# Both products of a decoder's MLP by Strassen's seven block products, with the activations between them kept in DRAM

## The chip, the cores and the metric

The kernel runs on one core of a Trainium2 chip. The metric is the device time of one execution in microseconds (us), the median of three runs; less is better.

## The reference

One layer of a decoder: model width 1024, 1024 tokens, hidden width 4096, all float32. The mixers at its front are the same before and after, and only what follows them matters here:

```
x = x + mix @ w_out                       # (1024,1024) @ (1024,1024)
h2 = rms_norm(x, norm2_g)
x = x + square(relu(h2 @ w_ff1)) @ w_ff2  # 1024x1024 @ 1024x4096, then 1024x4096 @ 4096x1024
```

## The kernel before

**Precision.** TensorE multiplies a reduced format, so each float32 operand is split in two: a "hi" part, a cast that ScalarE (ACT) does, and a "lo" part, the operand minus hi, a subtraction that VectorE (DVE) or GpSimd (POOL) does. Each product is three matmuls, hi by hi, lo by hi and hi by lo (`mm3`, L160 to L162). A matmul has a 128x128 stationary operand and a 128x512 moving one, and its result goes to a PSUM bank of 128x512.

**Output projection and second norm.** `wo_tile` makes a 128-token, 512-column tile of the projection in PSUM (`po`) and adds x. The first column half is done in two parts: seven of eight row blocks early, under the last attention unit, and the eighth at the end, added to what lies in SBUF. Then `norm_to_T` normalises the tile (a short chain of small operations), scales it (`n2sq`, L150), transposes it on TensorE (`n2tp`, L153) and splits it (ACT L156, DVE L157) into `h2Th`, `h2Tl`. Tokens come in eight tiles t; "half 0" is t of 0 to 3, "half 1" the rest. x1, the residual, stays in 16 SBUF tiles.

**MLP.** `ff1(fi, half)` makes one block of 128 hidden columns for 512 tokens: 8 by 3 matmuls into `pf`, relu and square on ACT (L947, L948), r times r and the lo part on DVE (L949, L950). `ff2(c)` takes two such blocks and makes 16 output tiles `py`, 6 matmuls each, that DVE adds into x1 (L963). First and second product alternate, chunk by chunk, 16 chunks in all; the first four blocks of half 0 (`EARLY`) have no use for half 1, and a scheduler that orders the program puts their matmuls between the last steps of the second norm. Weights come in 256 KB pieces on SP's queue (`w1raw`, `w2raw`); ACT makes hi (L119) and POOL lo (L122). The two products have 1536 matmuls each.

## Time and profile before

| | |
|---|---|
| median of 3 runs | 1412.03 us (1410.52 to 1413.05) |
| profiled execution, span | 1414.0 us |
| busy: TensorE (PE), DVE, ACT, POOL | 96%, 58%, 41%, 31% |
| last `po` matmul starts | 711.24 us |
| last `n2tp` transposes start | 723.70 us |

The span is that of one profiled execution, from its first instruction to its last, and is 2.0 us above the median of the timed runs. In rows of the profile a `start us, us, engine line op out<-in` gives start and duration; out and in are tiles by the program's names; brackets give how long the engine sat idle before it and what ended that. "PEclk" is the TensorE clock that was granted, 1.00 being full.

### The profile page before, as it was taken

To read this page: it belongs to the slowest core of one execution; us is meant where nothing else is said; L and a number is where in the kernel's file an instruction comes from. 1 tells how busy PE (TensorE), PEld (TensorE's weight loads), DVE (VectorE), ACT (ScalarE), POOL (GpSimd) and SP (SyncE) were. 2 spreads that over 40 slices of the span, in tenths; PEclk is the share of its full clock that TensorE was granted. 3 is DMA by queue.
4 is the path that set the end of the run, shared out by engine and by line. 5 is a ranking of instruction groups with operands and counts; after the bars stand their busy time and mean duration, and the time that the engine had idled before them with its cause. 6 is when DMAs were issued, how large, how long until landed. Compare 5 with 4: busy or idle time off the path is not lost.

```text
span 1414.0 us, 20140 instructions
## 1 busy us (share of the span) xinstructions
PE 1356.7 (96%) x7584; PEld 1133.8 (80%) x7584; DVE 816.6 (58%) x1623; ACT 578.1 (41%) x1401; POOL 442.0 (31%) x470
## 2 busy tenths in 40 slices
PE   4999989999999898899999999999999999999998
PEld 4978879878698795577888888888888888888887
DVE  6768657868676788968554434334343334334344
ACT  5566436867694457746442112221122211122111
POOL 6213684504126836211032222221122211222210
PEclk9999989999999998999999999999999999999999
DMA  8101220202002112313022112210122111122103
GB/s 222 41 17 28 48 47 16 60 23 60 23 9 68 29 41 77 118 52 98 31 75 60 35 55 60 60 46 30 45 60 60 51 32 43 54 60 60 40 21 119
DMA packets 107305, 76.89 MB, mean 54 GB/s; under 512 B 44220, under 2 KB 85180, under 8 KB 107208
## 3 DMA queue, kind: packets, MB, share of 16 engines
...
## 4 chain that ended last, share of the span: by engine, by line
PE 84%; DVE 8%; DMA 2%; ACT 2%; issue 2%; POOL 1%; SPq 0%; POOLq 0%; DVEq 0%; ACTq 0%
PE pf L162 8%; PE pf L161 8%; PE py L160 8%; PE py L161 8%; PE pf L160 8%; PE py L162 8%; PE pj L160 6%; PE pj L162 6%; PE pj L161 6%; PE av L459 3%; PE atp L440 2%; DVE sbr L398 2%; PE po L160 2%; PE po L161 2%; PE po L162 2%
## 5 line engine op out<-in xcount | busy, mean ns | idle before, releaser
L963 DVE TENSOR_TENSOR x<-py,x 128x512 f32<-128x512 f32 x256 | 176.1, 688 | 304.6 <-PE py L162 304.6
L122 POOL TENSOR_TENSOR w2lo<-w2raw,w2hi 128x512 fp32r<-128x512 f32 x64 | 81.9, 1303 | 440.9 <-ACT w2hi L119 440.9
L162 PE MATMUL pf<-h2Th,w1lo 128*128 128x512 f32 x512 | 199.3, 389 | 0.0
L160 PE MATMUL pf<-h2Th,w1hi 128*128 128x512 f32 x512 | 199.3, 389 | 0.0
L161 PE MATMUL pf<-h2Tl,w1hi 128*128 128x512 f32 x512 | 199.2, 389 | 0.0
L160 PE MATMUL pj<-whi,hTh 128*128 128x384 f32 (+2 forms) x512 | 172.5, 339 | 2.2 <-ACT vg L606 1.2
L161 PE MATMUL pj<-wlo,hTh 128*128 128x384 f32 (+2 forms) x512 | 171.7, 337 | 0.0
L162 PE MATMUL pj<-whi,hTl 128*128 128x384 f32 (+2 forms) x512 | 171.5, 336 | 0.0
L119 ACT CAST w2hi<-w2raw 128x512 fp32r<-128x512 f32 x64 | 36.5, 619 | 251.6 <-PE pf L161 171.9
L949 DVE TENSOR_TENSOR fr<-fr 128x512 f32<-128x512 f32 x64 | 65.8, 1028 | 106.1 <-ACT ah L948 89.8
L947 ACT ACTIVATE fr<-pf 128x512 f32<-128x512 f32 x64 | 38.0, 594 | 200.7 <-PE pf L162 200.7
L122 POOL TENSOR_TENSOR w1lo<-w1raw,w1hi 128x512 fp32r<-128x512 f32 x64 | 81.6, 1301 | 119.8 <-ACT w1hi L119 119.7
L160 PEld LDWEIGHTS pf<-h2Th,w1hi 128*128 128x128 f32 x512 | 96.2, 188 | 19.9
L162 PEld LDWEIGHTS pf<-h2Th,w1lo 128*128 128x128 f32 x512 | 96.1, 188 | 19.9
L161 PEld LDWEIGHTS pf<-h2Tl,w1hi 128*128 128x128 f32 x512 | 96.1, 188 | 19.9
L160 PEld LDWEIGHTS pj<-whi,hTh 128*128 128x128 f32 x512 | 99.2, 194 | 5.7 <-issue 1.7
L161 PEld LDWEIGHTS pj<-wlo,hTh 128*128 128x128 f32 x512 | 99.1, 194 | 2.5 <-issue 1.9
L352 POOL TENSOR_TENSOR qd<-qraw,qnr 128x128 f32<-128x128 f32 x96 | 47.7, 518 | 169.4 <-PE qtp L356 160.1
L162 PEld LDWEIGHTS pj<-whi,hTl 128*128 128x128 f32 x512 | 98.7, 193 | 2.3 <-issue 1.3
L161 PE MATMUL py<-w2lo,ah 128*128 128x512 f32 x256 | 99.6, 389 | 0.0
L162 PE MATMUL py<-w2hi,al 128*128 128x512 f32 x256 | 99.6, 389 | 0.0
L160 PE MATMUL py<-w2hi,a 128*128 128x512 f32 x256 | 99.6, 389 | 0.0
...
## 6 DMA issues: line engine op xcount, KB each, us to landing
w1raw<-in_w_ff_dram SPq DMA_DIRECT2D x64, 256.0 KB, 2.9
w2raw<-in_w_ff_dram SPq DMA_DIRECT2D x64, 256.0 KB, 3.0
...
wraw<-in_w_in_dram SPq DMA_DIRECT2D x16, 256.0 KB, 3.9
xraw<-in_x_dram SPq DMA_DIRECT2D x16, 256.0 KB, 2.8
cb<-c_dram SPq DMA_DIRECT2D x12, 256.0 KB, 3.3
...
mix_m<-ot ACTq DMA_DIRECT2D x10, 256.0 KB, 2.0
```

The costliest lines, as they stand in the source:

```text
L119: S.copy(hi, raw)
L122: lo_eng.tensor_tensor(out=lo, in0=raw, in1=hi, op=ALU.subtract)
L160: PE.matmul(o, lhsT=lh, rhs=rh, start=start, stop=False)
L161: PE.matmul(o, lhsT=lh, rhs=rl, start=False, stop=False)
L162: PE.matmul(o, lhsT=ll, rhs=rh, start=False, stop=stop)
L352: G.tensor_tensor(out=qd[:, :, e, :], in0=st["q"][half][:, ts, h, :], in1=st["r"][half][:, ts, h:h + 1].broadcast_to([P, 2, HD]), op=ALU.mult)
L398: V.tensor_tensor_scan(out=rv, data0=rv, data1=e[:, ::-1], initial=0.0 if prev is None else prev, op0=ALU.add, op1=ALU.add)
L440: PE.transpose(out=tp[:, j * P:(j + 1) * P], in_=a_of[c][:, j * P:(j + 1) * P], identity=ident)
L459: PE.matmul(o[h * HD:(h + 1) * HD, c0:], lhsT=st["v"][j // 4][:, j % 4, h, :], rhs=at[h][j // 4][:, j % 4, c0:], start=(j == 0), stop=(j = ...
L947: S.activation(r, p, AF.Relu)
L949: V.tensor_tensor(out=r, in0=r, in1=r, op=ALU.mult)
L963: V.tensor_tensor(out=x1[(t, ch)], in0=p, in1=x1[(t, ch)], op=ALU.add)
```

## The change

Each of the two MLP products is a 2x2 block product. Strassen's form with 15 sums needs seven block products instead of eight, and sums of blocks before and after them. Tile names change accordingly.

- **Count.** First product: 16 pairs q of hidden blocks, 7 products of 12 matmuls each. Second: 16 pairs q in groups of 1, 3, 4, 4 and 4; a group does its seven products one after the other (order 1, 6, 2, 7, 5, 4, 3), 4 token tiles by n pairs by 3 matmuls each. That is 1344 matmuls for each, 2688 in place of 3072.
- **x1** no longer stays in SBUF. The early part goes to DRAM (`x1p`) and comes back; the finished tiles go to `x1d` (writes on ACT's queue) and come back as 16 tiles `xo` at the start of the second product.
- **Second norm.** `to_ops` writes blocks b11, b21 for half 0 and forms differences with half 1 (four DVE operations for each tile, L978, L968, L971, L969). After the last tile, t1, t4 and b22 are split: 12 ACT casts and 12 DVE subtractions (L999, L1000).
- **First product** (`ff1`). For each q POOL does 4 sums of weight blocks (L1026) and 3 lo's, DVE 4 lo's and 5 additions from PSUM, ACT 7 casts, a copy, 4 relus, 4 squares. Two products, w11 by b11 and w12 by b21, run two pairs ahead. The result goes to DRAM (`yd`, 64 writes of 256 KB on SP's queue, L1040). The second product starts when the first is done.
- **Second product.** The activations (`yraw`) and weights (`w2raw`) come in 512 KB tiles on SP's queue (L1112), 8 buffers each, 4 KB a partition. Both operands of each product are split (`cut`): 2 ACT casts and 2 lo's for each q. In all POOL has 172 operations here (48 lo's L133, 60 additions of `u` into `xo` L1142, 64 sums L1160, L1163, L1165, L1185). DVE has 360: 176 lo's (L133) and 64 sums (L1162, L1164, L1166, L1186), which read two SBUF tiles, and 120 additions that read PSUM. ACT has 244. Split operands have 32 buffers, two products of a group of four.

PE at the end of the second norm. Before, around the transposes of the last two tiles (`pf` is the first MLP product):

```order
L162 MATMUL pf<-h2Th,w1lo 128x512
L160 MATMUL pf<-h2Th,w1hi 128x512
L161 MATMUL pf<-h2Tl,w1hi 128x512
L153 MATMUL n2tp<-ident,n2sq 128x128 x12
L162 MATMUL pf<-h2Th,w1lo 128x512
```

And now, the same place (`pa` is the first MLP product):

```order
L162 MATMUL n2tp<-ident,n2sq 128x128 x8
L173 MATMUL po<-woh,mTh 128x512
L174 MATMUL po<-wol,mTh 128x512
L175 MATMUL po<-woh,mTl 128x512
L162 MATMUL n2tp<-ident,n2sq 128x128 x16
L1033 MATMUL pa<-b11h,w11h 128x512
```

The first MLP product's matmuls stood ahead of the last transposes; now they stand behind them, and nothing is between the last `po` and those transposes.

ACT behind the same place. Now (L977, L964 and L973 belong to `to_ops`; `t_8748`, `t_8757` and `b_8766` are the hi parts of t1, t4 and b22; `w12h` is the second operand that PE needs):

```order
L977 COPY b_8721<-n2tp 128x512
L964 COPY hraw<-n2tp 128x4x128
L999 CAST t_8748<-hraw 128x512 x4
L973 CAST t_8482<-t2f 128x4x128
L973 CAST t_8483<-t3f 128x4x128
L999 CAST t_8757<-hraw 128x512 x4
L999 CAST b_8766<-hraw 128x512 x4
L130 CAST w12h<-w1raw 128x512
```

The casts of the last blocks stand ahead of `w12h`.

POOL at the start of the second product, now (`u` is a block product on its way to the output, `xo` the residual):

```order
L1160 TENSOR_TENSOR s_11222<-yraw 128x512
L1163 TENSOR_TENSOR yraw<-yraw 128x512
L1165 TENSOR_TENSOR yraw<-s_11222,yraw 128x512
L133 TENSOR_TENSOR fbl<-w2raw,fbh 128x512
L1185 TENSOR_TENSOR yraw<-yraw 128x512
L1142 TENSOR_TENSOR xo<-u,xo 128x512 x5
```

The additions into `xo` come early in POOL's order and need the residual back from DRAM. On SP's queue its 16 loads stand behind the last six writes of `yd` and the first four 512 KB loads, and the first addition takes the 13th of them. Of the next group's 16 loads those of `A[q, 1]` and `B[q, 1]` take buffers that this group's last two products still read.

The diff, its core; the MLP section before (`load_ff1` to the end) is removed whole:

```diff
-    sb = ctx.enter_context(tc.tile_pool(name="sb", bufs=1))
...
+    def pool(name, side=None, space=None):
+        kw = dict(space=space) if space else dict(side=side)
+        held[name] = ExitStack()
+        return held[name].enter_context(tc.tile_pool(name=name, bufs=1, reuse_waits="tile", **kw))
+    sb_w = pool("sb_w", "left")
+    sb_a = pool("sb_a", "right")
+    sb_t = pool("sb_t", "right")
+    ps = pool("ps", space=PSUM)
...
-            S.copy(hi[:, ks, sl], pv)
-            V.tensor_tensor(out=lo[:, ks, sl], in0=pv, in1=hi[:, ks, sl], op=ALU.subtract)
+            tT(t, c, p.rearrange("p (k t) -> p k t", t=P))
...
+    x1p = dr.tile([T, 512], F32, name="x1p")
+    x1d = dr.tile([T, D], F32, name="x1d")
     def wo_tile(ch, t, k0, k1):
...
+        ts, cs = slice(t * P, (t + 1) * P), slice(ch * 512, (ch + 1) * 512)
+        xr = big("raw", "xraw")
+        nc.sync.dma_start(out=xr, in_=xf[ts, cs] if k0 == 0 else x1p[ts])
+        if k1 < NK:
+            part = big("xt", "xpart")
+            V.tensor_tensor(out=part, in0=p, in1=xr, op=ALU.add)
+            nc.scalar.dma_start(out=x1p[ts], in_=part)
+        else:
+            x1[(t, ch)] = sb_h.tile([P, 512], F32, name="x1", tag="x1", bufs=4)
+            V.tensor_tensor(out=x1[(t, ch)], in0=p, in1=xr, op=ALU.add)
+            nc.scalar.dma_start(out=x1d[ts, cs], in_=x1[(t, ch)])
...
-        norm_to_T([x1[(t, 0)], x1[(t, 1)]], g2b, h2T, t, "n2")
...
+    held["sb_t"].close()
+    sb_h = pool("sb_h", "right")
...
+    def to_ops(t, c, pv):
+        sl = slice((t % 4) * P, (t % 4 + 1) * P)
+        raw = hraw[c][:, :, sl]
+        if t < 4:
+            hi, lo = (a[:, :, sl] for a in HB[("b11", "b21")[c]])
+            S.copy(hi, pv)
+            V.tensor_copy(raw, pv)
+            G.tensor_tensor(out=lo, in0=raw, in1=hi, op=ALU.subtract)
+            return
+        b22 = hraw[2][:, :, sl]
+        if c == 1:
+            if "t2" not in HB:
+                hop("t2", "a")
+                hop("t3", "a")
+            S.copy(b22, pv)
+            for name in ("t2", "t3"):
+                x = big("zs", name + "f", [P, 4, P])
+                if name == "t2":
+                    V.tensor_tensor(out=x, in0=b22, in1=hraw[0][:, :, sl], op=ALU.subtract)
+                    V.tensor_tensor(out=raw, in0=raw, in1=x, op=ALU.subtract)
+                else:
+                    V.tensor_tensor(out=x, in0=b22, in1=b12[0], op=ALU.subtract)
+                hi, lo = (a[:, :, sl] for a in HB[name])
+                S.copy(hi, x)
+                G.tensor_tensor(out=lo, in0=x, in1=hi, op=ALU.subtract)
+        else:
+            b12[0] = big("zs", "b12", [P, 4, P])
+            S.copy(b12[0], pv)
+            V.tensor_tensor(out=raw, in0=b12[0], in1=raw, op=ALU.subtract)
+    b12 = [None]
+    for t in TORD:
+        wo_tile(0, t, LAST, NK)
+        wo_tile(1, t, 0, NK)
+        norm_to_T([x1.pop((t, 0)), x1.pop((t, 1))], g2b, to_ops, t, "n2")
+    held["sb_w"].close()
+    sb_m = pool("sb_m", "left")
+    held["ps"].close()
+    pb = pool("pb", space=PSUM)
+    def bank(name):
+        return pb.tile([P, 512], F32, name=name, tag="b", bufs=8)
+    for name, raw, side in (("t1", hraw[0], "a"), ("t4", hraw[1], "a"), ("b22", hraw[2], "m")):
+        hop(name, side)
+        hi, lo = HB[name]
+        for k in range(4):
+            S.copy(hi[:, k], raw[:, k])
+            V.tensor_tensor(out=lo[:, k], in0=raw[:, k], in1=hi[:, k], op=ALU.subtract)
+    NPAIR = DFF // P // 2
+    yd = dr.tile([DFF, T], F32, name="yd")
+    AHEAD = 2
...
+    def ff1(q):
+        st = {}
+        def load():
+            home, n = (sb_h, 2) if q % 3 == 0 else (sb_m, 4)
+            st["w"] = [home.tile([P, 4, 2 * P], F32, name="w1raw", tag="wr", bufs=n) for _ in range(2)]
+            for c in range(2):
+                nc.sync.dma_start(out=st["w"][c], in_=w_ff1[c * 512:(c + 1) * 512, q * 2 * P:(q + 1) * 2 * P].rearrange("(k p) c -> p k c", p=P))
+        def blk(i, k):
+            return st["w"][k][:, :, i * P:(i + 1) * P]
+        def comb(name, a, b, op):
+            x = sb_m.tile([P, 4, P], F32, name=name, tag="s", bufs=4)
+            G.tensor_tensor(out=x, in0=a, in1=b, op=op)
+            return x
+        def prod(name, raw, b, eng, o, start=True, first=False):
+            wh, wl = pieces(raw, name, eng, sb_h if first else sb_m, 2 if first else 9)
+            bh, bl = HB[b]
+            for k in range(4):
+                PE.matmul(o, lhsT=wh[:, k], rhs=bh[:, k], start=start and k == 0, stop=False, skip_group_check=not start)
+                PE.matmul(o, lhsT=wh[:, k], rhs=bl[:, k], start=False, stop=False, skip_group_check=not start)
+                PE.matmul(o, lhsT=wl[:, k], rhs=bh[:, k], start=False, stop=k == 3, skip_group_check=not start)
+        def out(i, j, y):
+            f0 = (2 * q + i) * P
+            S.activation(y, y, AF.Square)
+            nc.sync.dma_start(out=yd[f0:f0 + P, j * 512:(j + 1) * 512], in_=y)
+        def one():
+            st["a"] = bank("pa")
+            prod("w11", blk(0, 0), "b11", V, st["a"], first=True)
+            st["c"] = sb_h.tile(BLK, F32, name="cc", tag="hraw", bufs=3)
+            S.copy(st["c"][:, 0], st["a"])
+            prod("w12", blk(0, 1), "b21", V, st["a"], start=False)
+            r = sb_m.tile([P, 512], F32, name="r", tag="r", bufs=1)
+            S.activation(r, st["a"], AF.Relu)
+            out(0, 0, r)
+        def two():
+            c = st["c"]
+            s1 = comb("s1", blk(1, 0), blk(1, 1), ALU.add)
+            s2 = comb("s2", s1, blk(0, 0), ALU.subtract)
+            b_ = bank("pb")
+            prod("s2", s2, "t2", G, b_)
+            V.tensor_tensor(out=c[:, 0], in0=b_, in1=c[:, 0], op=ALU.add)
+            s3 = comb("s3", blk(0, 0), blk(1, 0), ALU.subtract)
+            c_ = bank("pc")
+            prod("s3", s3, "t3", G, c_)
+            V.tensor_tensor(out=c[:, 1], in0=c_, in1=c[:, 0], op=ALU.add)
+            d_ = bank("pd")
+            prod("s1", s1, "t1", V, d_)
+            V.tensor_tensor(out=c[:, 1], in0=d_, in1=c[:, 1], op=ALU.add)
+            s4 = comb("s4", blk(0, 1), s2, ALU.subtract)
+            prod("w22", blk(1, 1), "t4", G, c_, start=False)
+            V.tensor_tensor(out=c[:, 2], in0=c_, in1=c[:, 0], op=ALU.add)
+            prod("s4", s4, "b22", V, d_, start=False)
+            V.tensor_tensor(out=c[:, 3], in0=d_, in1=c[:, 0], op=ALU.add)
+            for n, (i, j) in ((1, (1, 1)), (2, (1, 0)), (3, (0, 1))):
+                S.activation(c[:, n], c[:, n], AF.Relu)
+                out(i, j, c[:, n])
+        return load, one, two
+    steps = [ff1(q) for q in range(NPAIR)]
+    for q in range(AHEAD):
+        steps[q][0]()
+        steps[q][1]()
+    for q in range(NPAIR):
+        if q + AHEAD < NPAIR:
+            steps[q + AHEAD][0]()
+        steps[q][2]()
+        if q + AHEAD < NPAIR:
+            steps[q + AHEAD][1]()
+    held["sb_h"].close()
+    held["sb_a"].close()
+    held["sb_m"].close()
+    sb_f = pool("sb_f", "left")
+    GROUPS = (1, 3, 4, 4, 4)
+    GM = max(GROUPS)
+    X = {}
+    def ft(shape, name, tag, bufs, dt=F32):
+        return sb_f.tile(shape, dt, name=name, tag=tag, bufs=bufs)
+    q0 = 0
+    for gi, n in enumerate(GROUPS):
+        qs = range(q0, q0 + n)
+        q0 += n
+        last = gi == len(GROUPS) - 1
+        A, B = {}, {}
+        for q in qs:
+            for k in range(2):
+                for M, src, nm in ((A, yd, "yraw"), (B, w_ff2, "w2raw")):
+                    M[q, k] = ft([P, 2, 512], nm, nm, 2 * GM)
+                    f0 = (2 * q + k) * P
+                    nc.sync.dma_start(out=M[q, k].rearrange("p a b -> p (a b)"), in_=src[f0:f0 + P, :])
+        if gi == 0:
+            for j in range(2):
+                for i in range(2):
+                    for ti in range(4):
+                        X[ti, i, j] = ft([P, 512], "xo", "xo", 16)
+                        t = i * 4 + ti
+                        nc.sync.dma_start(out=X[ti, i, j], in_=x1d[t * P:(t + 1) * P, j * 512:(j + 1) * 512])
+        ops = {}
+        def cut(m, a, b):
+            for q in qs:
+                l, r = [], []
+                for to, x, nm, eng in ((l, a(q), "fa", V), (r, b(q), "fb", V if m in (1, 2, 5, 7) else G)):
+                    hi, lo = (ft([P, 512], nm + c, "fop", 8 * GM, F32R) for c in "hl")
+                    split(x, hi, lo, eng)
+                    to += [hi, lo]
+                ops[m, q] = l + r
+        def run(m, ti, o, start=True):
+            ts = slice(ti * P, (ti + 1) * P)
+            for q in qs:
+                lh, ll, rh, rl = ops[m, q]
+                kw = dict(skip_group_check=not start)
+                PE.matmul(o, lhsT=lh[:, ts], rhs=rh, start=start and q == qs[0], stop=False, **kw)
+                PE.matmul(o, lhsT=lh[:, ts], rhs=rl, start=False, stop=False, **kw)
+                PE.matmul(o, lhsT=ll[:, ts], rhs=rh, start=False, stop=q == qs[-1], **kw)
+        def add(ti, i, j, y, eng=V):
+            eng.tensor_tensor(out=X[ti, i, j], in0=y, in1=X[ti, i, j], op=ALU.add)
+        def done(ti, i, j):
+            if last:
+                t = i * 4 + ti
+                nc.sync.dma_start(out=outf[t * P:(t + 1) * P, j * 512:(j + 1) * 512], in_=X[ti, i, j])
+        s1, t1, pa, pc, pd, u = {}, {}, {}, {}, {}, {}
+        cut(1, lambda q: A[q, 0][:, 0], lambda q: B[q, 0][:, 0])
+        for ti in range(4):
+            pa[ti] = bank("pa")
+            run(1, ti, pa[ti])
+            u[ti] = ft([P, 512], "u", "u", 4)
+            S.copy(u[ti], pa[ti])
+        for q in qs:
+            s1[q] = ft([P, 512], "s1", "s1", GM)
+            G.tensor_tensor(out=s1[q], in0=A[q, 0][:, 1], in1=A[q, 1][:, 1], op=ALU.add)
+            t1[q] = ft([P, 512], "t1", "t1", GM)
+            V.tensor_tensor(out=t1[q], in0=B[q, 0][:, 1], in1=B[q, 0][:, 0], op=ALU.subtract)
+            G.tensor_tensor(out=A[q, 0][:, 1], in0=A[q, 0][:, 0], in1=A[q, 0][:, 1], op=ALU.subtract)
+            V.tensor_tensor(out=B[q, 0][:, 1], in0=B[q, 1][:, 1], in1=B[q, 0][:, 1], op=ALU.subtract)
+            G.tensor_tensor(out=A[q, 0][:, 0], in0=s1[q], in1=A[q, 0][:, 0], op=ALU.subtract)
+            V.tensor_tensor(out=B[q, 0][:, 0], in0=B[q, 1][:, 1], in1=t1[q], op=ALU.subtract)
+        cut(6, lambda q: A[q, 0][:, 0], lambda q: B[q, 0][:, 0])
+        for ti in range(4):
+            o = bank("pb")
+            run(6, ti, o)
+            V.tensor_tensor(out=u[ti], in0=o, in1=u[ti], op=ALU.add)
+            add(ti, 1, 1, u[ti], G)
+        cut(2, lambda q: A[q, 1][:, 0], lambda q: B[q, 1][:, 0])
+        for ti in range(4):
+            run(2, ti, pa[ti], False)
+            add(ti, 0, 0, pa[ti])
+            done(ti, 0, 0)
+        cut(7, lambda q: A[q, 0][:, 1], lambda q: B[q, 0][:, 1])
+        for ti in range(4):
+            pc[ti] = bank("pc")
+            run(7, ti, pc[ti])
+            add(ti, 1, 1, pc[ti])
+            add(ti, 1, 0, u[ti], G)
+        for q in qs:
+            G.tensor_tensor(out=A[q, 1][:, 0], in0=A[q, 1][:, 0], in1=A[q, 0][:, 0], op=ALU.subtract)
+            V.tensor_tensor(out=B[q, 1][:, 0], in0=B[q, 1][:, 0], in1=B[q, 0][:, 0], op=ALU.subtract)
+        cut(5, lambda q: s1[q], lambda q: t1[q])
+        for ti in range(4):
+            pd[ti] = bank("pd")
+            run(5, ti, pd[ti])
+            add(ti, 1, 1, pd[ti])
+            add(ti, 0, 1, u[ti], G)
+            done(ti, 1, 1)
+        cut(4, lambda q: A[q, 1][:, 1], lambda q: B[q, 1][:, 0])
+        for ti in range(4):
+            run(4, ti, pc[ti], False)
+            add(ti, 1, 0, pc[ti])
+            done(ti, 1, 0)
+        cut(3, lambda q: A[q, 1][:, 0], lambda q: B[q, 1][:, 1])
+        for ti in range(4):
+            run(3, ti, pd[ti], False)
+            add(ti, 0, 1, pd[ti])
+            done(ti, 0, 1)
```

More of the change, by code (lines that the diff above doesn't have):

```diff
@@ L140, in norm_to_T @@
         ss = small.tile([P, 2], F32, name=nm + "ss")
[L141 removed]
+        sq = [big("zs" if nm == "n2" else ("e", "r", "zs")[t % 3], nm + "sq") for _ in range(2)]
         for c in range(2):
@@ new lines, in hybrid_block, with pieces @@
+    NPAIR = DFF // P // 2
+    yd = dr.tile([DFF, T], F32, name="yd")
+    AHEAD = 2
+    def pieces(raw, name, eng, home, n):
+        hi, lo = (home.tile(raw.shape, F32R, name=name + c, tag="op", bufs=n) for c in "hl")
+        split(raw, hi, lo, eng)
+        return hi, lo
+    def ff1(q):
[54 more added lines that the diff above has]
+        return load, one, two
@@ L985 @@
+    held["pb"].close()
+    held["sb_f"].close()
+    held.clear()
 _INS = ["x", "lb_logits", "norm1_g", "w_in", "hg_norm_g", "sb_q_norm_g", "sb_k_norm_g", "fox_q_norm_g",
```

112 lines of the change are left out of this document (24 added, 88 removed), and 2 rows, old and new, of the table CFG.

## The prediction

> **What bounds the kernel now.** I read the page first: the busy shares and the chain of waits.
>
> ```profile
> span 1414.0 us, 20140 instructions
> PE 1356.7 (96%) x7584; PEld 1133.8 (80%) x7584; DVE 816.6 (58%) x1623; ACT 578.1 (41%) x1401; POOL 442.0 (31%) x470
> PE 84%; DVE 8%; DMA 2%; ACT 2%; issue 2%; POOL 1%; SPq 0%; POOLq 0%; DVEq 0%; ACTq 0%
> ```
>
> TensorE is busy 96% of the span and is 84% of the chain. Since a share is an average, I then read stretches (PE, weight load, DVE, ACT, POOL busy with counts, granted clock, DMA share, GB/s):
>
> ```profile
> 0.00:10.00 10.00, 0.00 (x0) 0.00 (x0) 2.20 (x20) 4.80 (x13) 8.33 (x30) 1.00 0.85 254
> 21.80:25.20 3.40, 3.40 (x14) 3.30 (x13) 2.26 (x7) 2.60 (x9) 0.12 (x1) 0.50 0.76 273
> 800.00:900.00 100.00, 100.00 (x443) 82.83 (x442) 39.85 (x56) 20.84 (x36) 23.22 (x18) 1.00 0.16 48
> 1300.00:1400.00 100.00, 100.00 (x443) 82.84 (x442) 40.31 (x58) 18.56 (x32) 17.82 (x14) 1.00 0.14 45
> 1400.00:1414.00 14.00, 10.19 (x45) 8.09 (x44) 5.57 (x9) 0.00 (x0) 0.00 (x0) 1.00 0.45 176
> ```
>
> In the MLP TensorE has no gap: 443 counted matmuls in 100 us, one each 0.226 us. The timeline of PE gives the same spacing, and where the MLP starts:
>
> ```profile
> 711.02 0.39 PE L161 MATMUL po<-wol,mTh 128*128 128x512 f32 x1
> 711.24 0.39 PE L162 MATMUL po<-woh,mTl 128*128 128x512 f32 x1
> 711.47 0.39 PE L160 MATMUL pf<-h2Th,w1hi 128*128 128x512 f32 x1
> ...
> 717.37 1.47 PE L153 MATMUL n2tp<-ident,n2sq 128*128 128x128 f32 x12
> ...
> 723.70 1.03 PE L153 MATMUL n2tp<-ident,n2sq 128*128 128x128 f32 x8
> ```
>
> Starts are 0.227 us apart (the 0.39 is pipelined). 3072 matmuls at 0.227 are 697 us, from 711.5 to 1410. So a removed matmul is worth 0.227 us, as long as the others still come without a gap. DVE is at 40 of 100 us, POOL at 18 to 23: what is added to them decides whether that holds.
>
> **What is removed.** 384 matmuls by 0.227 = 87.2 us. 2688 remain, 610.2 us, 305.1 for each product. Up to the last `po` matmul, ending its turn at 711.5, PE's order is the same. 24 new writes, of partial sums and x1, stand on ACT's queue; an issue there takes ACT 0.34 us:
>
> ```profile
> 1410.95 0.34 ACTq L965 DMA_DIRECT2D out_dram<-x  x1
> ```
>
> They fall into a stage where PE sets the pace, so I cost them at nothing; without that cover they would be 8 us of ACT.
>
> **The end of the second norm, +26 us to the dense stretch.** Before, `pf` matmuls ran while the last tiles were normalised. Now no first product can start until the last transposes are done. From the last `po` the chain is addition, normalisation, scaling, transposes:
>
> ```profile
> 713.21 0.69 DVE L833 TENSOR_TENSOR x<-po,xraw 128x512 f32<-128x512 f32 x1
> 720.40 1.42 DVE L150 SCALAR_TENSOR_TENSOR n2sq<-x,n2r,g2b 128x512 f32<-128x512 f32 x2
> ```
>
> The last transposes end at 723.70 + 1.03 = 724.7, 13.2 us after 711.5, and they were covered. Now the cover is gone, and the previous tile's four new DVE operations (L978, L968, L971, L969, at about 0.69) stand in the same queue: +2.8, so 16.0. Behind them ACT does two copies, 14 casts and then `w12h`, without which PE has only the 12 matmuls of w11. Durations by groups:
>
> ```profile
> L119 ACT CAST w2hi<-w2raw 128x512 fp32r<-128x512 f32 x64 | 36.5, 619 | 251.6 <-PE pf L161 171.9
> L122 POOL TENSOR_TENSOR w2lo<-w2raw,w2hi 128x512 fp32r<-128x512 f32 x64 | 81.9, 1303 | 440.9 <-ACT w2hi L119 440.9
> L963 DVE TENSOR_TENSOR x<-py,x 128x512 f32<-128x512 f32 x256 | 176.1, 688 | 304.6 <-PE py L162 304.6
> L949 DVE TENSOR_TENSOR fr<-fr 128x512 f32<-128x512 f32 x64 | 65.8, 1028 | 106.1 <-ACT ah L948 89.8
> L947 ACT ACTIVATE fr<-pf 128x512 f32<-128x512 f32 x64 | 38.0, 594 | 200.7 <-PE pf L162 200.7
> ```
>
> 17 by 0.61 = 10.4 us, 26.4 in all: PE is dense from 711.5 + 26, with 12 matmuls (2.7 us) already done. From below it is 13 (if the casts overlap the chain), from above 29 (if the 12 DVE lo's and w12's, queued behind the four operations, end last: 16 + 2 + 16 by 0.69). I take 26, the sum of the queue that I see.
>
> **First product, 305.** In a pair's 19.1 us (84 by 0.227) ACT has 16 operations by 0.62 = 9.9 us, POOL 7 by 1.30 = 9.1, DVE 9 by 0.69 = 6.2. All have half their time free, two products run two pairs ahead, so I take PE's time. After a pause the clock is granted at half, as in the row 21.80:25.20 (0.50 for 3.4 us): 1.7 us, and I add 1.3 for small waits. End: 711.5 + 26 + 305.1 - 2.7 + 3.0 = 1042.9.
>
> **Second product, 358 in place of 305.** Here POOL has 172 operations, 172 by 1.303 = 224 us, and DVE 360, 360 by 0.688 = 248 us. Each alone fits under 305. But the row of L949 says 1028 mean for an operation that reads two SBUF tiles, L963, which reads PSUM and one SBUF tile, stays at 688. Here is why, DVE's timeline and POOL's:
>
> ```profile
> 811.54 1.46 DVE L949 TENSOR_TENSOR fr<-fr 128x512 f32<-128x512 f32 x1 [0.38 <-ACT a L948]
> 813.03 0.69 DVE L950 TENSOR_TENSOR a<-fr,a 128x512 fp32r<-128x512 f32 x1
> ```
>
> ```profile
> 809.90 2.54 POOL L122 TENSOR_TENSOR w2lo<-w2raw,w2hi 128x512 fp32r<-128x512 f32 x2 [25.83 <-ACT w2hi L119]
> 813.21 1.67 POOL L122 TENSOR_TENSOR w2lo<-w2raw,w2hi 128x512 fp32r<-128x512 f32 x1 [0.76 <-ACT w2hi L119]
> ```
>
> The DVE operation starts inside POOL's, which ends at 812.44, and ends at 813.00, 0.56 later: nearly its whole work came after POOL let go. Then POOL starts at 813.21 inside DVE's next one, which ends at 813.72, and ends 1.16 later, at 814.88. So an operation of POOL and a DVE one with two SBUF inputs take turns, at 1.16 and 0.56 a turn. In the second product that is 172 by 1.16 + 240 by 0.56 = 199.5 + 134.4 = 334 us, more than PE's 305.
>
> The Trainium skill, "SBUF — State Buffer", Who interferes with whom, says the same of these two kinds and calls it an exclusive lock held for the whole instruction, while DVE with one SBUF input goes free. These rows agree that one waits for the other, and L963's 688 with the exemption; by whole instructions the demand would be the dearer rival's below.
>
> To 334 come the edges. The first loads wait for the last `yd` write: addition, relu, square, issue, 0.69 + 0.59, and about 0.6 and 0.4 for the last two, 2.3. The first addition into `xo` needs 4 tiles of 0.52 MB and 13 of 0.26 MB, 5.5 MB, at 254 GB/s (row 0.00:10.00) 21.7 us, so POOL is stuck until 24 us. By then 5 POOL and about 19 DVE turns are done, 16 us. At the other end the last product's 48 matmuls, 10.9, follow the last split. At the change of groups, loads whose buffers are free only in the last two products come late: 12 tiles, 6.3 MB, take 24.8 at 254 GB/s, and 2 products of 10.9 cover 21.8. I take 5 in all, most of it hidden by the queue of turns. 24 + 334 - 16 + 10.9 + 5 = 358. Below: 332 (next part); above: 410.
>
> **The end.** Last addition and output as before:
>
> ```profile
> 1410.23 0.69 DVE L963 TENSOR_TENSOR x<-py,x 128x512 f32<-128x512 f32 x1 [0.67 <-PE py L162]
> ```
>
> The last start, 1410.2, to the span's end is 3.8. Sum: 1042.9 + 358 + 3.8 = 1404.7 for a span. The profiled span was 2.0 above the median, so I forecast **1403 us** timed: of 87 saved, 23 go to the second norm's end (26 less 2.7), 53 to the second product, 3 to hiccups.
>
> **Rivals.**
> - *The turns do not add up* (1377). POOL and DVE wait anyway for operands, their turns meet seldom, and PE sets the pace. For it: in 800 to 900 POOL's 23 us and DVE's 40 cost PE nothing. Against it: demand here is several times that. Left is the gap while POOL waits for `xo`: POOL is stuck until 24, then has 14 operations of group 1 and 9 sums of group 2, 30 us, before product 6 of group 2; PE has 27 us of work till then. 305 + 27 = 332, and 1042.9 + 332 + 3.8 - 2.0 = 1377.
> - *Changes of group are exposed* (1418, slower). The 12 late tiles must land, then the splits follow, and no queue of turns hides it, since turns lack operands meanwhile. A full change costs 24.8 + 4 (issue, landing, split) - 21.8 = 7 to 8.5, there are two, and the one from 3 pairs to 4 costs 3: 20 in place of 5, 1418. It decides from 9 us over my 5, where the time is 1412. Against it, the time that a weight load takes to land (KB, us) and the DMA share of 0.16 in the MLP:
>
> ```profile
> w2raw<-in_w_ff_dram SPq DMA_DIRECT2D x64, 256.0 KB, 3.0
> ```
>
> - *Turns are held for whole instructions* (1453, slower). 172 by 1.303 + 240 by 0.688 = 389, less 19 before 24 us: 24 + 389 - 19 + 10.9 + 5 = 410, so 1455 - 2 = 1453. For it: queues in order, a late POOL addition holds the DVE addition on the same `xo` behind it. Against it: 0.56 and 1.16 in the rows. It makes the change slower from a demand of 344 on, 3% over my 334.
> - *The change saves no matmuls as it says*: excluded by the count in the order, 2688.
>
> **How the numbers follow.** Forecast (1394 to 1410) 0.36, no adding turns 0.24, exposed changes 0.22, whole instructions or something between 0.18. About 0.2%, 2.8 us, is what can be told from no change here: 1409.2 to 1414.8 is the same. Faster: 0.34 of the forecast's, all 0.24 of the first rival: 0.58. Same: 0.02 of the forecast and 0.06 of the exposed changes: 0.08. Slower: 0.34. The range goes from just below the first rival, 1374, to 1436, leaving out the upper half of the whole-instruction case; the forecast's own is 1394 to 1410.
>
> **What would show it.** In the profile after: the last `po` at 711; PE idle between the transposes and `w12h`, ending near 737; `pa` to `pd` matmuls 0.227 apart with POOL and DVE under 60% busy until 1043; then a second product in which PE is busy about 85%, POOL's mean is above 1.3 us and that of DVE's L133 well above 0.69, and PE's waits name DVE and POOL lo's. PE at 95% there says first rival; gaps of 7 us or more at three places, ended by `yraw` loads, the second. Wrong altogether if the first product is not dense.

## The result: 3.5% slower, and the profile after

The changed kernel takes 1463.95 us (median of four, 1458.9 to 1465.6) against 1412.54 of the kernel before in the same comparison: a ratio of 1.035, 95% interval 1.0327 to 1.0373. The forecast was 1403 and its range ended at 1436. The profiled execution has a span of 1462.3 us; the prediction's own sum for a span was 1404.7, so 57.6 us have to be found.

The page of the changed kernel, its busy shares and the engines on its chain of waits:

```profile
span 1462.3 us, 20560 instructions
PE 1316.6 (90%) x7200; PEld 1082.2 (74%) x7200; DVE 1029.2 (70%) x1763; ACT 729.7 (50%) x1665; POOL 731.3 (50%) x642
PE 7%; DVE 6%; issue 2%; POOL 2%; DMA 1%; ACT 0%; DVEq 0%; ACTq 0%; POOLq 0%
```

PE's chain was 84% of the span before. Now PE and DVE have nearly equal shares of it (they sum to 18%: the chain could be followed back over the last part of the span only). 384 matmuls are gone, and PE's busy time has fallen by 40 us, not by 87. Stretches of the changed kernel (PE, weight load, DVE, ACT, POOL busy with counts, granted clock, DMA share, GB/s) show where:

```profile
720.00:740.00 20.00, 9.37 (x28) 6.95 (x28) 15.94 (x26) 10.82 (x24) 7.62 (x6) 0.50 0.25 79
740.00:755.00 15.00, 2.02 (x5) 1.08 (x6) 15.00 (x11) 5.89 (x11) 13.37 (x9) 0.61 0.12 35
800.00:850.00 50.00, 50.00 (x220) 41.05 (x219) 18.68 (x25) 24.61 (x41) 22.15 (x17) 1.00 0.35 111
1062.40:1458.80 396.40, 339.93 (x1344) 268.58 (x1344) 354.47 (x361) 133.31 (x246) 281.45 (x172) 0.91 0.30 107
1160.00:1180.00 20.00, 14.22 (x50) 10.93 (x49) 20.00 (x19) 3.23 (x6) 20.00 (x13) 0.82 0.39 127
```

The first product is dense, as forecast: 220 matmuls in 50 us at full clock. The end of the second norm (first two rows) is a hole in PE, with DVE busy all of the last 15 us. The second product is the fourth row, whole: its 1344 matmuls need 305 us when dense and take 396.4, while DVE is busy 354.5 of them. In the last row DVE and POOL are both busy without a gap and PE is not.

Against the terms of the sum:

| | forecast | measured | difference |
|---|---|---|---|
| last `po` starts | 711.24 | 716.44 | +5.2 |
| from its end (0.27 us later) to the dense first product | 26.0 | 38.0 | +12.0 |
| first product, dense part and small waits | 305.4 | 307.7 | +2.3 |
| second product, to the end of its last addition | 358.7 | 396.4 | +37.7 |
| from there to the end of the span | 3.1 | 3.5 | +0.4 |
| sum | | | +57.6 |

The first product is counted to the end of the addition behind it, at 1062.4; the forecast's 358 and 3.8 stand with the last addition, 0.69, moved from the one to the other.

**Second product.** Groups of DVE instructions in it (busy us, mean ns of one), those that read two SBUF tiles, and one of those that read PSUM (`fa` and `fb` are the two split operands of a product, `h` and `l` at the end of a name its hi and lo part):

```profile
L133 DVE TENSOR_TENSOR fal<-yraw,fah 128x512 fp32r<-128x512 f32 x96 | 111.2, 1172 | 16.5 <-ACT fah L130 16.3
L133 DVE TENSOR_TENSOR fbl<-w2raw,fbh 128x512 fp32r<-128x512 f32 x48 | 71.5, 1491 | 0.0
L1142 DVE TENSOR_TENSOR xo<-pd,xo 128x512 f32<-128x512 f32 x40 | 26.9, 682 | 15.0 <-PE pd L1139 15.0
...
L1166 DVE TENSOR_TENSOR w2raw<-w2raw,t 128x512 f32<-128x512 f32 x16 | 22.5, 1408 | 0.0
L133 DVE TENSOR_TENSOR fal<-s,fah 128x512 fp32r<-128x512 f32 x16 | 21.7, 1355 | 0.0
L133 DVE TENSOR_TENSOR fbl<-t,fbh 128x512 fp32r<-128x512 f32 x16 | 19.3, 1204 | 0.0
L1162 DVE TENSOR_TENSOR t<-w2raw 128x512 f32<-128x512 f32 x16 | 17.5, 1094 | 1.3 <-DMA w2raw<-in_w_ff_dram 1.2
L1186 DVE TENSOR_TENSOR w2raw<-w2raw 128x512 f32<-128x512 f32 x16 | 16.8, 1050 | 0.0
L1164 DVE TENSOR_TENSOR w2raw<-w2raw 128x512 f32<-128x512 f32 x16 | 16.1, 1007 | 4.0 <-POOL s L1160 2.6 <-DMA w2raw<-in_w_ff_dram 1.3
```

An addition from PSUM still takes 0.68. Every kind that reads two SBUF tiles takes 1.0 to 1.5. What they take above 0.69, summed over the eight rows (96 by 0.48, 48 by 0.80, 16 by 0.72 and so on), is 133 us: DVE stood at an instruction while POOL worked. Without that, DVE's 360 instructions are 221 us. So the 396.4 us are, on DVE, **221 of its own work, 133 of waiting behind POOL, and 42 idle**. POOL's groups in the same stretch:

```profile
L1142 POOL TENSOR_TENSOR xo<-u,xo 128x512 f32<-128x512 f32 x60 | 99.8, 1697 | 7.9 <-DVE u L1171 7.9
L133 POOL TENSOR_TENSOR fbl<-w2raw,fbh 128x512 fp32r<-128x512 f32 x48 | 78.4, 1655 | 45.8 <-ACT fbh L130 39.3 <-DVE fal L133 4.8 <-DMA xo<-x1d 1.7
```

1.30 before, 1.66 to 1.70 now. The turns one by one, DVE's timeline:

```profile
1151.17 0.68 DVE L1142 TENSOR_TENSOR xo<-pa,xo 128x512 f32<-128x512 f32 x1
1151.78 1.18 DVE L133 TENSOR_TENSOR fbl<-t,fbh 128x512 fp32r<-128x512 f32 x1
1152.88 0.68 DVE L1142 TENSOR_TENSOR xo<-pa,xo 128x512 f32<-128x512 f32 x1
1153.48 1.17 DVE L133 TENSOR_TENSOR fal<-s,fah 128x512 fp32r<-128x512 f32 x1
```

The two-input operations start 1.70 us apart (1151.78, 1153.48), with a PSUM addition between them. The forecast's turn of POOL and turn of DVE were 1.16 + 0.56 = 1.72. The price of a pair was right. The Trainium skill, "SBUF — State Buffer", Who interferes with whom, has a DVE operation with two SBUF inputs contend with a POOL operation that reads SBUF, as these rows do, and calls the shared pair an exclusive lock. Two whole instructions, 1.30 + 0.69, would be 1.99 a pair by my estimate, which is not what is measured.

What PE waits for in the second product, in all, times, longest:

```profile
PE pd L1138 <- DVE fbl L133: 11.5, 5, 4.1
PE pa L1137 <- ACT fbh L130: 8.9, 1, 8.9
PE pc L1138 <- DVE fbl L133: 8.9, 7, 2.4
PE pa L1138 <- DVE fbl L133: 8.5, 4, 2.9
```

DVE's lo's come late, as the prediction's last part asked; the one wait of 8.9 is the start, before anything has been loaded.

**End of the second norm.** PE's timeline, from the last `po`:

```profile
716.44 0.40 PE L175 MATMUL po<-woh,mTl 128*128 128x512 f32 x1
723.20 1.94 PE L162 MATMUL n2tp<-ident,n2sq 128*128 128x128 f32 x8 [6.36 <-DVE n2sq L159]
731.50 1.94 PE L162 MATMUL n2tp<-ident,n2sq 128*128 128x128 f32 x8 [6.37 <-DVE n2sq L159]
734.12 0.80 PE L1033 MATMUL pa<-b11h,w11h 128*128 128x512 f32 x1 [0.68 <-ACT hraw L964]
...
743.35 0.50 PE L1033 MATMUL pa<-b21h,w12h 128*128 128x512 f32 x1 [3.75 <-ACT cc L1046]
...
754.73 0.79 PE L1035 MATMUL pa<-b21h,w12l 128*128 128x512 f32 x1 [9.63 <-DVE w12l L133]
```

The chain to the last transposes is 731.5 + 1.9 - 716.7 = 16.7, forecast 16.0. `w12h` did not end last: with the copy `cc` that stands behind it on ACT, and that the row names, it let PE go at 743.35, 26.6 us after. What ends last is `w12l`, DVE's lo of the same weights, at 754.7. DVE there:

```profile
736.57 10.83 DVE L1000 TENSOR_TENSOR t<-hraw,t 128x512 fp32r<-128x512 f32 x7
747.32 6.75 DVE L1000 TENSOR_TENSOR b<-hraw,b 128x512 fp32r<-128x512 f32 x4
754.00 0.68 DVE L133 TENSOR_TENSOR w12l<-w1raw,w12h 128x512 fp32r<-128x512 f32 x1
```

and POOL:

```profile
740.04 1.74 POOL L1026 TENSOR_TENSOR s<-w1raw 128x512 f32<-128x512 f32 x1
...
746.80 1.72 POOL L133 TENSOR_TENSOR s2l<-s,s2h 128x512 fp32r<-128x512 f32 x1
```

Eleven lo's in 17.6 us, 1.6 each, beside POOL's sums of weights at 1.7. The same turns again, in a place where I had counted 0.69.

### The profile page after: what moved, and what is told of

Same layout as the page of the kernel before. It is cut to its first block, busy times and chain, and to the rows that moved or that the text cites. A ratio compares the mean times of both kernels' runs of the same rounds, so it can differ in the third digit from the quotient of the medians.

```text
span 1462.3 us, 20560 instructions
## 1 busy us (share of the span) xinstructions
PE 1316.6 (90%) x7200; PEld 1082.2 (74%) x7200; DVE 1029.2 (70%) x1763; ACT 729.7 (50%) x1665; POOL 731.3 (50%) x642
## 5 line engine op out<-in xcount | busy, mean ns | idle before, releaser
L130 ACT CAST fah<-yraw 128x512 fp32r<-128x512 f32 x96 | 59.5, 620 | 167.2 <-PE pc L1138 69.2
L133 DVE TENSOR_TENSOR fal<-yraw,fah 128x512 fp32r<-128x512 f32 x96 | 111.2, 1172 | 16.5 <-ACT fah L130 16.3
L1142 POOL TENSOR_TENSOR xo<-u,xo 128x512 f32<-128x512 f32 x60 | 99.8, 1697 | 7.9 <-DVE u L1171 7.9
L133 POOL TENSOR_TENSOR fbl<-w2raw,fbh 128x512 fp32r<-128x512 f32 x48 | 78.4, 1655 | 45.8 <-ACT fbh L130 39.3
L411 DVE TENSOR_TENSOR_SCAN sbr<-sbr,sbe 128x128 f32<-128x128 f32 (+3 forms) x72 | 78.3, 1093 | 10.3 <-ACT sbe L407 9.6
L133 POOL TENSOR_TENSOR wlo<-wraw,whi 128x384 fp32r<-128x384 f32 (+2 forms) x56 | 58.1, 1065 | 37.0 <-ACT whi L130 23.5
L133 DVE TENSOR_TENSOR fbl<-w2raw,fbh 128x512 fp32r<-128x512 f32 x48 | 71.5, 1491 | 0.0
L130 ACT CAST fbh<-w2raw 128x512 fp32r<-128x512 f32 x96 | 59.4, 618 | 20.6 <-DVE w2raw L1166 16.1
L472 PE MATMUL av<-at,vst 128*64 128x256 f32 x480 | 67.9, 367 | 1.6 <-ACT at L457 0.9
L1026 POOL TENSOR_TENSOR s<-w1raw 128x512 f32<-128x512 f32 x32 | 43.1, 1346 | 50.5 <-DVE s1l L133 49.4
L457 ACT COPY at<-atp 128x128 f32<-128x128 f32 (+3 forms) x120 | 56.4, 480 | 10.4 <-PE atp L453 9.1
```

The source lines that it names most:

```text
L130: S.copy(hi, raw)
L133: lo_eng.tensor_tensor(out=lo, in0=raw, in1=hi, op=ALU.subtract)
L411: V.tensor_tensor_scan(out=rv, data0=rv, data1=e[:, ::-1], initial=0.0 if prev is None else prev, op0=ALU.add, op1=ALU.add)
L457: S.copy(dst, tv)
L472: PE.matmul(o[h * HD:(h + 1) * HD, c0:], lhsT=st["v"][j // 4][:, j % 4, h, :], rhs=at[h][j // 4][:, j % 4, c0:], start=(j == 0), stop=(j = ...
L1142: eng.tensor_tensor(out=X[ti, i, j], in0=y, in1=X[ti, i, j], op=ALU.add)
```

## The experiments

The theory that the first four runs were written down with was still the prediction's: the turns of POOL and DVE, as a resource of their own, bound the second product, and the end of the second norm waits for DVE's lo's, which take turns as well. Its rivals were DVE's own queue and late loads at the start and at changes of group. The third run came out above the theory's range and below its rivals', and since then the theory is another: DVE's queue, which goes in order, bounds the second product, at its own work plus what it waits behind POOL. PE's clock is a rival that no run changed by itself. Where no number of runs is given, a time is that of a single run. A table of the second product in all kernels stands behind the runs.

**POOL's additions into `xo` left out**:

```diff
-            add(ti, 1, 1, u[ti], G)
...
-            add(ti, 1, 0, u[ti], G)
...
-            add(ti, 0, 1, u[ti], G)
```

> The changed kernel without POOL's 60 additions of u into xo in the second product (that part of the output is left out). Theory, turns of DVE and POOL bound the second product: 60 by 1.16 = 70 us of turns go, 264 are left, less than PE's 305, so the second product falls from 396 to 335 to 350 and the time from 1464 to 1405 to 1420; DVE's L133 falls to under 1.0 us mean. Rival, DVE's own queue is the bound (360 operations and their waits for operands): DVE loses nothing, time above 1450. Rival, late loads at the change of groups: 1445 or more, since the loads stand where they stood.

Its output lacks these parts. Measured 1413.71, 50 us less than the changed kernel, all of it in the second product:

```profile
1062.40:1408.90 346.50, 318.09 (x1344) 256.11 (x1344) 308.79 (x361) 133.51 (x246) 180.79 (x112) 0.97 0.33 122
```

60 POOL operations less take 45 us off DVE's busy time (354 to 309), though DVE has the same 360 operations. So POOL's work is paid for on DVE. The time lies in the theory's range; the rival's, by a DVE that loses nothing, began at 1450.

**All of POOL's work in the second product done by DVE:**

```diff
-... (r, b(q), "fb", V if m in (1, 2, 5, 7) else G)):
+... (r, b(q), "fb", V)):
...
-            G.tensor_tensor(out=s1[q], in0=A[q, 0][:, 1], in1=A[q, 1][:, 1], op=ALU.add)
+            V.tensor_tensor(out=s1[q], in0=A[q, 0][:, 1], in1=A[q, 1][:, 1], op=ALU.add)
...
-            add(ti, 1, 1, u[ti], G)
+            add(ti, 1, 1, u[ti])
```

and so on for the other three sums and two additions.

> All 172 POOL operations of the second product moved to DVE. Theory, turns: DVE then has 532 operations at a step of 0.60, 319 us, and waits for nobody: second product about 350, time 1410 to 1430, no DVE operation there over 0.75 us. Rival, DVE's own queue is the bound: 172 more operations make it 100 us longer, 1540 or more. Rival, late loads: at most 10 us either way.

Measured 1410.87: 53 us faster than the changed kernel with 172 more operations on DVE and a POOL without any. The stretch, and groups of DVE:

```profile
1062.80:1405.70 342.90, 315.72 (x1344) 255.24 (x1344) 321.39 (x533) 137.29 (x246) 0.00 (x0) 0.97 0.34 123
```

```profile
L133 DVE TENSOR_TENSOR fal<-yraw,fah 128x512 fp32r<-128x512 f32 x96 | 65.5, 683 | 9.3 <-ACT fah L130 8.8 <-DMA xo<-x1d 0.3
L1142 DVE TENSOR_TENSOR xo<-u,xo 128x512 f32<-128x512 f32 x60 | 39.3, 684 | 0.0
```

532 operations in 321 us, 0.60 each, no group above its usual duration: the waits are gone with POOL. The rival, by which DVE only gets 172 operations more to do, had 1540 or more.

**Only the additions of `u` left on POOL** (the other 112 operations on DVE). By turns it needs 60 by 1.16 + 352 by 0.56 = 267 us, as little as without these additions above (264), while DVE has 112 operations more than there.

> POOL keeps only the 60 additions of u; its 48 lo's and 64 sums of the second product go to DVE. Theory, turns: 60 by 1.16 + 352 by 0.56 = 267 us of turns, DVE's own queue 472 by 0.60 = 283, both under PE's 305: second product 335 to 350, time 1400 to 1420. Rival, DVE's own queue: 112 more operations, 1520 or more. Rival, late loads at the change of groups: 1440 to 1464.

Measured 1435.13 (two runs; ratio to before 1.0144, interval 1.0114 to 1.0173), above the theory's range of 1400 to 1420 and below that of either rival.

```profile
1065.20:1430.10 364.90, 322.34 (x1344) 258.91 (x1344) 336.99 (x472) 133.33 (x246) 102.54 (x60) 0.95 0.32 116
```

By turns it should have been PE's time. It is 18 us longer than the first experiment, whose turns are the same, and so is DVE: 337 busy in place of 309. What I wrote down for this run still took the turns' sum for the bound where it is smaller; the run ended that. DVE's busy time, waits in it, is what counts.

**The first MLP weights split ahead of t1, t4 and b22:** the loop that makes them stands behind the two first products instead of ahead of them.

```diff
-    for name, raw, side in (("t1", hraw[0], "a"), ("t4", hraw[1], "a"), ("b22", hraw[2], "m")):
...
     for q in range(AHEAD):
         steps[q][0]()
         steps[q][1]()
+    for name, raw, side in (("t1", hraw[0], "a"), ("t4", hraw[1], "a"), ("b22", hraw[2], "m")):
...
```

> The two products that run ahead (w11, w12 of the first two pairs) written ahead of the splitting of t1, t4 and b22, so that four of DVE's lo's and four of ACT's casts move behind those of w12. Theory, PE's wait at the end of the second norm (739.5 to 754.7) is for w12's lo behind DVE's 12 lo's, which take turns with POOL at 1.69 us each: four of them fewer ahead, 7 us: time 1455 to 1459. Rival, PE waits for the blocks t1 to t4 anyway: within 2 us of 1464.

Measured 1459.98, 4 us less; the changed kernel's own four runs lie within 7. The wait for `w12l` fell from 9.63 to 5.51:

```profile
751.42 0.79 PE L1029 MATMUL pa<-b21h,w12l 128*128 128x512 f32 x1 [5.51 <-DVE w12l L133]
```

That is the order of the program, and the scheduler still put some of these lo's ahead of it. The end of the norm does wait for DVE's queue: from the last `po` to the last matmul of the first product it is 340.5 us in place of 344.9. In the time of the kernel a gain of this size is hardly above what single runs differ by.

**All on DVE, and the start of the second product freed:** `yd` is written by ACT's queue, the first group's tiles lie where b11 and b21 were, so that they load during the last products, and `xo` comes in the order of its use.

```diff
-            nc.sync.dma_start(out=yd[f0:f0 + P, j * 512:(j + 1) * 512], in_=y)
+            nc.scalar.dma_start(out=yd[f0:f0 + P, j * 512:(j + 1) * 512], in_=y)
...
+            B[0, 1] = ft([P, 2, 512], "w2raw", "w1b", 1)
+            A[0, 0] = ft([P, 2, 512], "yraw", "y1a", 1)
...
-            for j in range(2):
-                for i in range(2):
+            for i, j in ((1, 1), (0, 0), (1, 0), (0, 1)):
```

> On top of the kernel with the second product's POOL work on DVE (1411): the writes of yd go to ACT's queue, the first pair's four tiles lie where b11 and b21 were, so that their loads start before the first product ends, and xo is loaded in the order of its use. Theory: the start of the second product (PE waits 9 us for the first split and 18 us more for operands and additions held behind the 16 loads of xo) is the largest wait left, and most of it goes: 1390 to 1400. Rival, the start is bound by DVE's work, which is the same: 1405 to 1411.

Measured 1407.91 (seven runs, ratio 0.9954, interval 0.9935 to 0.9972): 3 us less than the single run without it, not 10 to 20, and its own seven runs lie between 1403.84 and 1410.25. PE's first wait fell from 8.9 to 3.6, but then DVE is full at once while loads run at 409 GB/s:

```profile
1080.00:1100.00 20.00, 13.38 (x40) 7.89 (x39) 20.00 (x34) 5.37 (x9) 0.00 (x0) 0.81 1.03 409
```

So the start is bound by DVE, whose first groups (1 and 3 pairs) have the most additions for each matmul; the loads had cost no more than the few us that came back.

**The same, with the end of the second norm in another order:** the splits of t1, t4 and b22 are held back until the last w12 has been split, the two lo's of the last tile go to DVE, and `cc` of the first pair lies in tiles of its own.

```diff
-                G.tensor_tensor(out=lo, in0=x, in1=hi, op=ALU.subtract)
+                (G if t < 7 else V).tensor_tensor(out=lo, in0=x, in1=hi, op=ALU.subtract)
...
+    cast, sub_ = LASTW["w12"]
+    with tc.issue_after(cast.ins), tc.issue_after(sub_.ins):
+        for name, raw, side in (("t1", hraw[0], "a"), ("t4", hraw[1], "a"), ("b22", hraw[2], "m")):
```

> As e5_early_loads, and at the end of the second norm the splits of w11 and w12 stand ahead of those of t1, t4 and b22 on ACT and DVE, the first pair's running sum has a buffer of its own, and the last tile's two lo's are on DVE, so that POOL's sums come earlier. Theory, PE's second wait there (739 to 755) is DVE's queue of 12 lo's that take turns with POOL: PE is dense 8 to 14 us earlier, time 1378 to 1390. Rival, PE then waits as long for t2 and s2: within 4 us of e5_early_loads.

Measured 1403.42 (three runs, ratio 0.9926, interval 0.9885 to 0.9968): 4.5 us less than the run above, where 8 to 14 were expected. From the last `po` to the last matmul of the first product it is 337.9 us in place of 345.0 in the run above. The wait for `w12l` is gone, and the next two stand there, with another behind the transposes' scaling:

```profile
739.22 1.09 PE L162 MATMUL n2tp<-ident,n2sq 128*128 128x128 f32 x4 [8.20 <-DVE n2sq L159]
...
755.99 0.50 PE L1029 MATMUL pb<-t,s2h 128*128 128x512 f32 x1 [2.03 <-ACT s2h L130]
758.99 0.80 PE L1031 MATMUL pb<-t,s2l 128*128 128x512 f32 x1 [2.27 <-POOL s2l L133]
```

**Second product by eight block products in the changed frame** (1536 matmuls, no sums of blocks, 128 lo's and 256 additions on DVE):

```diff
-        cut(1, lambda q: A[q, 0][:, 0], lambda q: B[q, 0][:, 0])
...
+                    for k in range(2):
+                        ah, al = op["fa", k, i]
+                        wh, wl = op["fb", k, j]
+                        mm3(o, ah[:, ts], al[:, ts], wh, wl, k == 0, k == 1)
+                    V.tensor_tensor(out=X[ti, i, j], in0=o, in1=X[ti, i, j], op=ALU.add)
```

> The changed kernel with the second product undone to eight plain block products (1536 matmuls, 128 splits on DVE, no sums, no POOL; x1 and the activations still through DRAM). Theory: this product was bound by turns and not by PE, so that 192 more matmuls cost nothing: 1536 by 0.227 = 349 us, 9 us at the start, against 396: time 1420 to 1432. Rival, PE sets the pace there: 192 by 0.227 = 44 us longer, 1508.

Measured 1426.78: 192 more matmuls than the changed kernel, and 37 us faster.

```profile
1061.50:1421.60 360.10, 351.49 (x1536) 290.19 (x1536) 247.04 (x385) 75.66 (x130) 0.00 (x0) 0.99 0.34 117
```

Here PE sets the pace again. As this kernel has it, the first product by seven, with all that it costs around it, doesn't pay on its own either: 1426.78 against 1412.36 before.

**The changed kernel with the order of the norm's end alone:**

> The changed kernel with only the end of the second norm reordered as in e6_tail_order; the second product as changed. Theory: 8 to 14 us of the 1464 go, 1450 to 1456, all before 760 us of the span. Rival, PE then waits as long for t2 and s2: 1460 or more.

Measured 1456.9, 7 us less than the changed kernel, but not where it was expected. From the last `po` to the last matmul of the first product it is 337.6 us in place of 344.9, as in the run with both orders; the last `po` itself came 5.4 us later, at 721.79, so that 2 us are left. The other 5 us lie in the second product, 391.2 in place of 396.4, which is written the same in both. So profiles of second products written the same differ by 5 us.

**All on DVE, both orders, and four groups of four pairs** (the 1 and 3 merged; loads half by half, in tags by half):

```diff
-    GROUPS = (1, 3, 4, 4, 4)
+    GROUPS = (4, 4, 4, 4)
...
-                    M[q, k] = ft([P, 2, 512], nm, nm, 2 * GM)
+                (A, B)[m][q, k] = ft([P, 2, 512], ("yraw", "w2raw")[m], "raw%d" % k, 2 * GM)
```

> As e6_tail_order, with groups of 4, 4, 4 and 4 pairs in place of 1, 3, 4, 4, 4 (36 DVE additions fewer, 496 operations in all) and the loads by halves, the first half of them into tiles that are free before the first product ends. Theory, DVE's own queue is what the second product waits for in its first 60 us (a group of one pair has 36 additions by 0.60 = 21.6 us and 13 us of splits and sums against 19 us of PE): DVE then has 298 us, under PE's 305, and the time is 1373 to 1385. Rival, the start waits for loads (12 MB before the second group) whatever the groups: 1392 or more.

Measured 1382.51 (four runs, 1381.21 to 1385.15; before in the same comparison 1415.41; ratio 0.9772, interval 0.9743 to 0.9801). It beats both kernels.

```profile
1059.80:1378.30 318.50, 308.97 (x1344) 252.54 (x1344) 299.76 (x497) 131.47 (x242) 0.00 (x0) 0.99 0.35 124
```

One group less is 36 fewer additions (496 operations), DVE falls from 321 us to 300, under PE's 305, and the stretch from 338.5, in the run with both orders, to 318.5, within 13.5 us of PE's dense time. The loads and some buffers changed in the same run, so that the 20 us are not shown to come from the additions alone, though DVE lost 22. The longest that are left of its waits, in all, times, longest:

```profile
PE pb L1156 <- ACT fbh L130: 4.8, 4, 1.8
PE pa L1156 <- ACT fbh L130: 3.6, 1, 3.6
```

**The same, with the last tiles' four differences behind the next tile's scaling:**

> As e9_groups_of_four, and at the end of the second norm each tile's four DVE differences stand behind the next tile's scaling. Theory, the last two tiles' transposes (10 us apart in e6_tail_order) wait for DVE's queue and not for the chain of small operations: the last transposes come 4 to 6 us earlier after the last po, and the time is 3 to 6 us below e9_groups_of_four. Rival, the chain of small operations sets it: within 1.5 us.

Measured 1381.01 (four runs, 1377.76 to 1385.8, ratio 0.977, interval 0.9732 to 0.9809): not to be told from the run above. The transposes did come sooner:

```profile
716.03 0.40 PE L177 MATMUL po<-woh,mTl 128*128 128x512 f32 x1
...
723.94 1.94 PE L164 MATMUL n2tp<-ident,n2sq 128*128 128x128 f32 x8 [5.99 <-DVE n2sq L159]
```

The last of them start 7.9 us behind the last `po`, where it was 18.6 in the run above (739.70 and 721.10). But then PE waits 4.4 for `w12l`, 3.5 for `s2h` and 1.4 for `s2l`, and the first product ends as far behind the last `po` as before, 337.3 and 337.6 us. DVE has the same work to do, and only the place of the wait has moved.

**The changed kernel with loads by half** (buffers of each half apart, so that the next group's first halves load two products sooner):

```diff
-        for q in qs:
-            for k in range(2):
+        for k in range(2):
+            for q in qs:
...
-                    M[q, k] = ft([P, 2, 512], nm, nm, 2 * GM)
+                    M[q, k] = ft([P, 2, 512], nm, "raw%d" % k, 2 * GM)
```

> The changed kernel with the loads of each group in two halves, each with buffers of its own, the half that the first products read first. Theory, turns on DVE's queue: at most 3 us for each of the three large changes of group, 1455 to 1464. Rival, late loads at the change of groups cost 8 us each beside the turns: 1440 or less.

Measured 1457.77, 6 us less than the changed kernel's median and 1 less than the fastest of its runs. Its second product takes 390.5 us, and that of the kernel with the norm's order alone, whose loads are as they were, takes 391.2. So no gain is shown; late loads at the changes of group cost at most 6 us.

The second product in all of them, in us ("waits" is DVE's time above 0.68, their mean where POOL has no work, in operations with two SBUF inputs; "own" is the rest of its busy time):

| kernel | length | PE busy | DVE operations | own | waits | idle | POOL operations | waits by POOL operation |
|---|---|---|---|---|---|---|---|---|
| changed | 396.4 | 339.9 | 360 | 221 | 133 | 42 | 172 | 0.77 |
| loads by half | 390.5 | 335.8 | 360 | 220 | 135 | 35 | 172 | 0.79 |
| order of the norm's end | 391.2 | 336.7 | 360 | 221 | 132 | 38 | 172 | 0.77 |
| first weights split ahead | 394.1 | 337.4 | 360 | 222 | 133 | 39 | 172 | 0.78 |
| without `u` into `xo` | 346.5 | 318.1 | 360 | 220 | 88 | 38 | 112 | 0.79 |
| `u` alone on POOL | 364.9 | 322.3 | 472 | 287 | 50 | 28 | 60 | 0.84 |
| all on DVE | 342.9 | 315.7 | 532 | 321 | 0 | 22 | 0 | |
| the same, start freed | 338.6 | 319.9 | 532 | 321 | 0 | 17 | 0 | |
| the same, both orders | 338.5 | 318.1 | 532 | 321 | 0 | 17 | 0 | |
| groups of four | 318.5 | 309.0 | 496 | 300 | 0 | 19 | 0 | |
| the same, differences behind | 318.7 | 309.1 | 496 | 300 | 0 | 19 | 0 | |
| eight block products | 360.1 | 351.5 | 384 | 247 | 0 | 113 | 0 | |

In every row but the last DVE is busy for 89 to 95% of the stretch, and the length goes with its queue to within the idle time, 17 to 42 us. It doesn't follow exactly: without `u` into `xo` DVE has 12 us less to do than with all on DVE, and the stretch is 4 longer. In the groups of four PE is busy for 97% as well, so that both engines are near their limit. **Each operation given to POOL cost DVE 0.77 to 0.84 us of waiting on average, where DVE does the same operation itself in 0.60.** In this stretch POOL takes nothing off DVE.

## Why the prediction was wrong, point by point

- **Matmuls removed, 0.227 us each.** Right where PE is dense (the first product). In the second product the 192 removed matmuls bought nothing, since another engine set the pace. The sign of the forecast hung on this.
- **Last `po`, "PE's order is the same": off by 5.2.** Stretches of the changed kernel around the last attention unit:

```profile
650.00:660.00 10.00, 7.38 (x40) 5.41 (x40) 6.31 (x18) 6.12 (x14) 1.28 (x1) 0.83 0.52 160
660.00:670.00 10.00, 7.56 (x41) 5.52 (x37) 3.52 (x8) 3.97 (x11) 0.00 (x0) 0.83 0.39 120
```

  PE was busy 8.8 and 9.9 of 10 us here before, at a clock of 1.00. In the twelve profiles with the changed front the last `po` came between 716.0 and 722.3, never at 711. Kernels whose front is written the same differ in it by 4 us (716.3 to 720.3), and of the kernel before there is one profile, so that the size is uncertain too. What moved there (partial sums through DRAM, the order around the last attention unit) was not taken apart; the cause stays open.
- **End of the second norm, 26: off by 12.** The chain, 16.0, was right (16.7). The queue behind it was taken from ACT (17 by 0.61); the one that ended last was DVE's, which I had put into the upper bound of 29 at 0.69 an operation. With POOL's weight sums beside them eleven lo's took 1.6 each. I had used the turns in the second product and not here. To have them in another order is worth 4.4, 7.1 and 7.3 us from the last `po` to the end of the first product (three comparisons), not all 12, since waits for `s2h`, `s2l` and the scaling take their place.
- **First product, 305.4: right (307.7).** ACT, POOL and DVE are busy for half of the stretch shown or less, PE without a gap.
- **Second product, 358: off by 37.7.** The step that failed is "172 by 1.16 + 240 by 0.56 = 334". The prices were right (1.70 a pair), the sum was of the wrong thing. It adds up what the shared resource is held for; but the resource is not what comes last, DVE's queue is, and this queue also carries 120 PSUM additions, 72 us by 0.60, to which the sum gave no time. Some of them run while POOL has its turn, as the four rows of the timeline show; DVE's 354 busy less 334 says that about 20 us did not fit. The other 17 are edges: DVE idled 42 us and I had allowed 24 (24 - 16 + 10.9 + 5). The run with `u` alone on POOL shows that this is more than a size: its turns are fewer than PE's 305, and it still ran 365.
- **The start, 24 us until the first addition into `xo`: too dear,** 19 us (1081.45 - 1062.4), as loads ran at 394 to 408 GB/s and not at 254. To load sooner gained 3 us: DVE was full there in any case.
- **The end, 3.8 from the start of the last addition: right (1462.3 - 1458.1 = 4.2).**
- **Rivals.** *Turns held for whole instructions* (1453, at 0.18; its own terms add up to 1455, since the 2.0 between span and time were taken off twice) came nearest in time, but that is luck: a pair takes 1.70 and not 1.99, and what makes it dear is the queue behind it. *Turns don't add up* (1377) falls: the waits are 133 us. *Changes of group exposed* (1418): with loads by half at most 6 us come back, where profiles of second products written the same differ by 5 and this rival needed 9 over my 5. That the merged first groups gain by fewer additions on DVE, and not by their loads, is argued and not shown.
- **What could have been read before:** the prediction's own row of L949 took 1.46 beside a POOL operation and not 0.69, a wait of 0.77, which is what each POOL operation cost here on average. That the two agree so well is luck: in the timeline above single operations take 1.17 and 1.18, a wait of 0.49, and others just ahead of them 1.77 and 1.78. 360 by 0.60 + 172 by 0.77 = 348 for DVE's queue, and with the 24 of edges 372: 14 more than 358, 1417 in place of 1403, and no longer a gain, though still 47 short of the time measured. The rest of the miss, the idle time and the end of the norm, was not in it.
